# First layer's down projection as seven half-size products; weight sums spread two at a time; three norms from sums by token

## The chip, the cores and the metric

The kernel runs on one core of one Trainium2 chip. The metric is device time in microseconds; the kernel before took 1694.76 us (median of three runs, 1693.58 to 1695.71). Matrix products run on TensorE (PE), elementwise work on VectorE (DVE), ScalarE (ACT) and GpSimd (POOL); weights come in through DMA queues that SyncE (SP), POOL and ACT feed.

## What is computed

Two layers over 512 tokens of width 1024, in float32:

```python
for l in range(DEPTH):                      # DEPTH = 2
    h = rmsnorm(x, norm1_g[l])
    p = h @ w_in[l]                         # split for three branches and their gates
    y_rw, y_ret, y_sg = rwkv7(...), retention(...), spatial_gating(...)
    x = x + sum(gates * branch_projections) @ w_out[l]          # "output projection"
    u = rmsnorm(x, norm2_g[l]) @ ffn_w_up[l]                    # "up projection", 2 * 2816 columns
    c = causal depthwise convolution of width 3 over u
    gate, val = split(c)
    x = x + (silu(gate) * val) @ ffn_w_down[l]                  # "down projection", K = 2816
return rmsnorm(x, final_g)
```

## The kernel before, in words

The activations lie with channels on the 128 partitions and the 512 tokens along the free dimension. Every large product is made of float32 values split in two parts of a reduced format, `hi` and `lo` (one ACT copy and one DVE subtraction each, `part`, lines 140 and 141), and of three matmuls per 128 x 128 block (`mm3`, lines 153 to 163): `hi*lo`, `hi*hi`, `lo*hi`. Weights come as units of at most 128 x 512 elements (256 KB), read by SP (`load`, line 127), split by `part`, and used by TensorE. `unit` walks a plan of all units in advance: it reads up to `NRAW` or `DEEP` units ahead and splits as many ahead as `AHEAD` gives for the unit's pool. A scheduler orders the instructions of each engine from its own timing model, except where `keep_in_program_order` pins them (`self.pin` for matmuls, `self.keep` for splits and norms).

The stages of a layer are: the mixer (three branches), the output projection (`wout`: eight row blocks `m`, each 8 x 3 matmuls of 512 columns, then `xi`, the residual sum, and the norm's pieces `norm_z` and `norm_sq`), the up projection (`ffn_up`: 44 columns of 8 x 3 matmuls, each followed by the scaling with the norm's factor row `rsF`, the convolution and the gate) and the down projection.

The second layer's down projection (`last`) is computed with seven products of half the size in each dimension (a Strassen scheme): the activations are combined by `halves` in the up projection, and the weight blocks by `presum`: four DMA loads of `wdt` on POOL's queue into `pre` tiles, four DVE sums, four DMA stores to DRAM (`ts`), which `last` reads back as units. Four of the seven products use such sums. `presum` for the second layer runs during the up and down projection of the first. The first layer's down projection (`ffn_down`, lines 1146 to 1160) is a plain product: for each of eight row blocks 22 x 3 matmuls of 512 columns, with the activations split by `split`.

A norm needs the sum of squares over channels of each token. For the first norm of the program this is done by `norm_stats` (four matmuls with one output column, a DVE step, a POOL power, giving the factor by token) and `norm_rows` (four transposes on TensorE and one ACT copy, giving the row `rsF`). The other three norms use `norm_bcast` (lines 282 to 300): the squares are split, two matmuls of 512 columns with a matrix of ones sum and spread them, and ACT's square root and four DVE reciprocals give `rsF`; for the second layer's first norm a DVE transpose and POOL copies also give the factor by token. `firstF` (lines 318 to 330) places it: three columns are begun with the first half of the channels, then the norm, then the second halves.

Of the kernel before, what the change touches and what calls it, by code (L numbers as in the profile page):

```python
# [8 lines left out]
F32 = mybir.dt.float32  # L9
# [6 lines left out]
L = 2  # L16
# [10 lines left out]
PRE = {(0, "f", 2): 0, (0, "f", 4): 1, (0, "f", 6): 2, (0, "f", 8): 3, (0, "d", 0): 4, (0, "d", 1): 5, (0, "d", 2): 6, (0, "d", 3): 7,  # L27
       (0, "d", 4): 8, (0, "d", 5): 9, (0, "d", 6): 10}
# [24 lines left out]
class Emit:  # L53
# [41 lines left out]
    def unit(self, name, l, i, c0, n=512):  # L95
# [9 lines left out]
        while self.npart < len(self.plan):  # L105
# [6 lines left out]
            while self.nraw < len(self.plan) and self.nraw < self.npart + (DEEP if self.plan[self.nraw][5] in ("q", "u") else NRAW):  # L112
                self.load(self.plan[self.nraw])
# [8 lines left out]
    def load(self, u):  # L122
        name, l, i, c0, n, _ = u
        raw = self.u(n="wr") if u[5] in ("q", "u") and self.nraw % 2 else self.wp.tile([128, 512], F32, name=self.nm("wr"), tag="wr", bufs=NRAW)
        src = self.tsum[i] if name == "tsum" else self.a[name][l, i]
        with self.tc.high_priority():
            self.kept(self.nc.sync.dma_start(raw[:, :n], src[:, c0:c0 + n]))
        self.raws.append(raw)
        self.nraw += 1

    def part(self, u):
# [5 lines left out]
        else:  # L137
            hi, lo = [{"f": self.f, "r": self.r, "u": self.u, "p": self.u, "q": self.u}[pool](dt=F32R, n=t) for t in ("sh", "sl")]
# [104 lines left out]
    def presum(self, l, stage, m):  # L243

        if self.pre:
            q, b = self.pre.pop()
            V = self.nc.vector
            V.tensor_tensor(b[3], b[3], b[1], op=SUB)
            V.tensor_tensor(b[1], b[1], b[0], op=SUB)
            V.tensor_tensor(b[0], b[0], b[3], op=ADD)  # L250
            V.tensor_tensor(b[2], b[2], b[0], op=SUB)
            for p, t in zip((7, 5, 6, 4), (b[3], b[1], b[0], b[2])):
                self.tsum[q, p] = self.dp.tile([128, 512], F32, name=self.nm("ts"))
                self.nc.gpsimd.dma_start(self.tsum[q, p], t)
        q = PRE.get((l, stage, m))
        if q is not None:
            b = self.fpre.pop(0) if stage == "f" else [self.u(n="pre") for _ in range(4)]
            for i, t in enumerate(b):
                self.nc.gpsimd.dma_start(t, self.a["wdt"][0, 2 * q + i // 2][:, i % 2 * 512:i % 2 * 512 + 512])
            self.pre.append((q, b))  # L260
# [20 lines left out]

    def norm_bcast(self, st, cols):

        nc, po = self.nc, self.tc.keep_in_program_order
        hi, lo = st["sq"]
        pb = self.sm()
        po(nc.tensor.matmul(pb, self.ones, lo, start=True, stop=False))
        po(nc.tensor.matmul(pb, self.ones, hi, start=False, stop=True))
        rms = self.u(n="rms")
        nc.scalar.activation(rms, pb, AF.Sqrt, scale=1.0 / D, bias=self.c("eps"))  # L290
        self.rsF = self.small((128, 512), "rsF", bufs=1)
        for c in range(NC):
            cs = slice(c * 128, c * 128 + 128)
            nc.vector.reciprocal(self.rsF[:, cs], rms[:, cs])
        if cols:
            t = self.u((128, 4, 4, 32), n="rst")
            nc.vector.transpose(t.rearrange("p c b r -> p (c b r)"), self.rsF)
            self.rsT = self.small((128, 4), "rs")
            for b in range(4):
                nc.gpsimd.tensor_copy(self.rsT[32 * b:32 * b + 32, :], t[32 * b:32 * b + 32, :, b, 0])  # L300
# [1166 lines left out]
```

## Time and profile before

| | |
|---|---|
| median of three runs | 1694.76 us |
| the profiled execution | 1695.1 us |
| span of its profile | 1693.4 us |
| TensorE matmuls | busy 1683.6 us (99%), 10247 instructions |
| TensorE weight loads | busy 1382.6 us (82%), overlapping the matmuls |
| VectorE | busy 1218.0 us (72%) |
| ScalarE | busy 794.9 us (47%) |
| GpSimd | busy 261.8 us (15%) |
| DMA | 260.01 MB, mean 154 GB/s |

A matmul's duration in the profile runs from its issue to its modelled end, so consecutive matmuls overlap in the records; what a matmul costs in a stream is the distance between two starts. In the rows, `a<-b,c` names the result first, then the streamed operand and the loaded weights; `128x512` is the shape of the result. Times in windows and timelines count from the span's start.

The places on TensorE, from the timeline: the first layer's output projection is interleaved with the last of the mixer and ends near 494.6 us, its norm's sum stands at 506.7 us; the first down projection ends near 854.3 us, with the norm's sum at 862.3 us; the second layer's `xi` rows run from before 1321.7 to 1343.8 us and its norm's sum stands at 1353.7 us; the last down projection runs to 1687 us.

### The profile page before, as it was taken

Reading aid. Unit: us, or ns where it says so; the run is one execution under the profiler, and the core shown is the slowest. Engines: PE = TensorE matmul, PEld = TensorE weight load, DVE = VectorE, ACT = ScalarE, POOL = GpSimd, SP = SyncE. Lnnn points to the kernel's source line nnn. Section 1 sums busy time; section 2 is a strip of 40 time slices with the busy share of each in tenths; the row PEclk is TensorE's granted clock in tenths of the full one; section 3 lists DMA queues with packets and bytes.
Section 4 is the critical chain, followed back from the end, with each engine's and each line's share of the span. In section 5 each row is a group of like instructions: output and inputs, shape, how many; then the busy total and the mean of one; then the engine's idle time right before and its main releaser. Section 6 shows DMA issues by size and latency. Waiting matters only on the chain.

```text
span 1693.4 us, 27939 instructions
## 1 busy us (share of the span) xinstructions
PE 1683.6 (99%) x10247; PEld 1382.6 (82%) x10247; DVE 1218.0 (72%) x2114; ACT 794.9 (47%) x1366; POOL 261.8 (15%) x376
## 2 busy tenths in 40 slices
PE   9999999999999999999999999999999999999998
PEld 7888877888888888888888888778888888888887
DVE  7887745578669877655568888465786688887777
ACT  6563543554255444433346544335542544444555
POOL 1121000303301200003321210003132012220000
PEclk9999999999999999999999999999999999999999
DMA  5236553625544533147743265536255434443775
GB/s 182 87 108 204 181 176 96 191 84 163 190 144 149 193 125 94 63 146 265 246 147 95 94 206 184 178 98 190 83 164 165 153 97 143 143 140 112 242 241 178
DMA packets 143529, 260.01 MB, mean 154 GB/s; under 512 B 19584, under 2 KB 35584, under 8 KB 143392
## 3 DMA queue, kind: packets, MB, share of 16 engines
q1 hardware_dynamic: 117200, 188.67, 35.5%
q0 software_dynamic: 17552, 54.15, 9.8%
q10 hardware_dynamic: 8640, 15.42, 2.5%
q8 instruction: 80, 1.31, 0.3%
q14 instruction: 57, 0.47, 0.1%
HBM read 212.94 MB, written 45.22 MB: 152 GB/s over the span
## 4 chain that ended last, share of the span: by engine, by line
PE 94%; issue 4%; DVE 1%; DMA 0%; POOL 0%; ACT 0%; DVEq 0%; POOLq 0%; ACTq 0%
PE acc L157 85%; PE sm L157 3%; PE sm L683 2%; PE sm L937 1%; PE sm L590 1%; PE sm L1045 0%; PE acc L351 0%; PE sm L553 0%; PE sm L552 0%; PE sm L965 0%; PE sm L992 0%; DMA s<-wl 0%; PE sm L837 0%; DVE wl L141 0%; PE sm L828 0%
## 5 line engine op out<-in xcount | busy, mean ns | idle before, releaser
L157 PE MATMUL acc<-lo,sh 128*128 128x512 f32 x1108 | 431.9, 390 | 0.0
L157 PE MATMUL acc<-hi,sh 128*128 128x512 f32 x1108 | 431.9, 390 | 0.0
L157 PE MATMUL acc<-hi,sl 128*128 128x512 f32 x1108 | 424.8, 390 | 0.0
L140 ACT CAST sh<-wr 128x512 fp32r<-128x512 f32 (+1 forms) x375 | 226.6, 614 | 298.9 <-PE acc L157 163.0
L141 DVE TENSOR_TENSOR sl<-wr,sh 128x512 fp32r<-128x512 f32 (+1 forms) x375 | 253.5, 683 | 99.8 <-ACT sh L140 70.1
L141 DVE TENSOR_TENSOR wl<-wr,wh 128x512 fp32r<-128x512 f32 x238 | 169.4, 715 | 145.2 <-ACT wh L140 142.2
L140 ACT CAST wh<-wr 128x512 fp32r<-128x512 f32 x238 | 146.8, 619 | 243.7 <-PE acc L157 151.8
L157 PEld LDWEIGHTS acc<-lo,sh 128*128 128x128 f32 x1108 | 208.0, 188 | 43.7 <-issue 0.9
L157 PEld LDWEIGHTS acc<-hi,sl 128*128 128x128 f32 x1108 | 208.1, 188 | 43.6 <-DVE gth L1060 0.3
L157 PEld LDWEIGHTS acc<-hi,sh 128*128 128x128 f32 x1108 | 208.1, 188 | 43.3 <-issue 0.3
L157 PE MATMUL acc<-lo,wh 128*128 128x512 f32 x588 | 231.7, 394 | 0.0
L157 PE MATMUL acc<-hi,wl 128*128 128x512 f32 x588 | 229.8, 391 | 0.0
L157 PE MATMUL acc<-hi,wh 128*128 128x512 f32 x588 | 229.2, 390 | 0.0
L1111 ACT ACTIVATE cv<-fu,pc 128x512 f32<-128x512 f32 x88 | 71.7, 816 | 139.4 <-DVE fu L1109 139.3
L157 PEld LDWEIGHTS acc<-hi,wl 128*128 128x128 f32 x588 | 110.4, 188 | 24.7 <-issue 0.9
L157 PEld LDWEIGHTS acc<-lo,wh 128*128 128x128 f32 x588 | 110.4, 188 | 24.3 <-ACT wh L140 0.6
L157 PEld LDWEIGHTS acc<-hi,wh 128*128 128x128 f32 x588 | 110.4, 188 | 22.4 <-issue 0.2
L157 PE MATMUL acc<-ah,sh 128*128 128x512 f32 x352 | 108.3, 389 | 0.0
L1112 DVE SCALAR_TENSOR_TENSOR cv<-fu,pc,cv 128x511 f32<-128x511 f32 x88 | 65.9, 750 | 34.8 <-ACT cv L1111 33.9
L157 PE MATMUL acc<-wl,hi 128*128 128x512 f32 x212 | 85.8, 405 | 0.0
L1109 DVE TENSOR_TENSOR fu<-acc,rsF 128x512 f32<-128x512 f32 x88 | 60.4, 686 | 31.8 <-PE acc L157 30.8
L157 PE MATMUL acc<-wh,hi 128*128 128x512 f32 x212 | 82.5, 389 | 0.0
(359 smaller groups left out, 2448.1 us busy)
## 6 DMA issues: line engine op xcount, KB each, us to landing
wr<-wall SPq DMA_DIRECT2D x480, 256.0 KB, 2.8
gd<-gth ACTq DMA_DIRECT2D x48, 256.0 KB, 3.2
gth<-gd POOLq DMA_DIRECT2D x48, 256.0 KB, 3.3
pre<-wdt POOLq DMA_DIRECT2D x44, 256.0 KB, 5.6
ts<-pre POOLq DMA_DIRECT2D x44, 256.0 KB, 2.8
wr<-ts SPq DMA_DIRECT2D x44, 256.0 KB, 4.2
wr<-wdn SPq DMA_DIRECT2D x40, 256.0 KB, 3.9
wr<-wdt SPq DMA_DIRECT2D x33, 256.0 KB, 4.2
```

Source lines behind the costliest of these rows:

```text
L140: self.kept(self.nc.scalar.copy(hi[:, :n], raw[:, :n]))
L141: self.kept(self.nc.vector.tensor_tensor(lo[:, :n], raw[:, :n], hi[:, :n], op=SUB))
L157: i = self.nc.tensor.matmul(*x, **y, **kw)
L590: i = T.matmul(pK[hv[1 - h], j, :], bk[hv[h], c, 1, :], x[hv[h], c, :], start=True, stop=True)
L683: po(T.matmul(o, l, r, start=start, stop=True, skip_group_check=True))
L937: po(T.matmul(X[h][:, i, :], lhsT, rhs, start=new[h], stop=stop, skip_group_check=True))
L1109: V.tensor_tensor(u, ps, self.rsF, op=MUL)
L1111: A.activation(t, u, AF.Identity, scale=self.p("cw2", j), bias=self.p("cb", j))
L1112: V.scalar_tensor_tensor(t[:, 1:], u[:, :511], self.p("cw1", j), t[:, 1:], op0=MUL, op1=ADD)
```

## The change

1. The first layer's down projection becomes seven products of half size. The weights stay the loaded operand; each matmul streams 256 columns. The results are added into the residual tiles `x[m]` in place, in halves of 256 columns.
2. `presum` becomes a generator `sums` for each layer, stepped two sums at a time in the output projection (`m` 1 to 6) and the up projection (`i` 0 to 15) of the same layer; the first layer needs it now too.
3. `halves` is used in both layers' up projections, and splits and norms there are pinned in both. The code that reads back the combined activations (`kit`) is shared by both.
4. `norm_bcast` is gone: the three norms use `norm_stats` and, two steps later in `firstF`, `norm_rows`.
5. Units of the output projection get the pool `w` and those at the end of the first down projection the pool `k`: half of the raw tiles come from the pool `f`, and more of them are read and split ahead.

```diff
-AHEAD = {None: 2, "p": 4, "r": 3, "f": 3, "u": 5, "q": 4}
+WOS, UPS = range(1, 7), range(16)
+AHEAD = {None: 2, "p": 4, "r": 3, "f": 3, "u": 5, "q": 4, "k": 5, "w": 3}
...
+    def sums(self, l):
+        V, P, Q = self.nc.vector, self.nc.gpsimd, NFF // 2
+        def get(q):
+            b = [self.f(n="pre") for _ in range(4)]
             for i, t in enumerate(b):
+                P.dma_start(t, self.a["wdt"][l, 2 * q + i // 2][:, i % 2 * 512:i % 2 * 512 + 512])
+            return b
+        b = get(0)
+        yield
+        for q in range(Q):
+            n = get(q + 1) if q < Q - 1 else None
+            for p, o, x, op in ((7, 3, 1, SUB), (5, 1, 0, SUB), (6, 0, 3, ADD), (4, 2, 0, SUB)):
+                V.tensor_tensor(b[o], b[o], b[x], op=op)
+                self.tsum[l, q, p] = self.dp.tile([128, 512], F32, name=self.nm("ts"))
+                P.dma_start(self.tsum[l, q, p], b[o])
+                if p == 5:
+                    yield
+            b = n
+            yield
...
         for i, g in enumerate(gs + gs):
             if i == at:
-                self.norm_bcast(st, l and ids[0] == 12)
+                self.norm_stats(st)
+            elif i == at + 2:
+                self.norm_rows()
             next(g)
...
     def wout(self, l, mg, xd, st):
+        self.sum, self.pool = self.sums(l), "w"
+        self.presum()
         for m in range(8):
...
+            self.presum(m in WOS)
+        self.pool = "r"
...
         for i in range(NFF):
-            if l == 0 and i % 2 == 0 and 2 <= i <= 10:
-                self.presum(l, "f", i)
+            self.presum(i in UPS)
...
-            if l < L - 1:
-                act.append(self.split(th, at))
-            elif i % 2 == 0:
+            if i % 2 == 0:
                 even = th
             else:
                 pair = [even, th]
...
     def ffn_down(self, l, act, x, st):
-        for m in range(8):
-            ps = self.acc()
-            self.matF(ps, ("wdn", l, m, 0), act)
-            V.scalar_tensor_tensor(x[m], ps, 0.5, x[m], op0=MUL, op1=ADD)
-            self.norm_z(st, x[m], "n1")
-            self.norm_sq(st, x[m])
...
+        def prod(ps, x, at, w, first, end, ms=range(4)):
+            for m in ms:
+                c = slice(128 * m, 128 * m + 128)
+                self.mm3(ps[m // 2][:, H[m % 2]], (w[0][:, c], w[1][:, c]), (x[0][:, at:at + 256], x[1][:, at:at + 256]),
+                         first and m % 2 == 0, end, skip_group_check=True)
+        def plus(m, h, ps, i):
+            V.scalar_tensor_tensor(x[m][:, H[h]], ps[i // 2][:, H[i % 2]], 0.5, x[m][:, H[h]], op0=MUL, op1=ADD)
...
+        for q in range(Q):                                   # Q = 11
+            for p in (7, 5, 6, 4) if q < Q - 1 else (6, 7, 5, 4):
+                w = unit(p, q)
+                side(n)
+                n += 1
+                xs, at = {7: (t, 0), 5: (s, 0), 6: (s, 256), 4: (t, 256)}[p]
+                prod(pss[p], xs, at, w, q == 0, q == Q - 1)
...
+        for q in range(Q):
+            w = unit(1, q)
+            rest(q)
+            prod(out[1], ab[q], 0, w, False, q == Q - 1)
...
+        for q in range(Q):
+            w = unit(2, q)
+            prod(out[2], ab[q], 256, w, q == 0, q == Q - 1)
...
+        for q in range(Q - KEPT):                            # KEPT = 6
+            w = unit(3, q)
+            prod(out[3], s4[q // 2], q % 2 * 256, w, q == 0, False)
...
+            if q:
+                norm(q - 1)
+        self.pool = "k"
+        ws = [unit(3, q) for q in range(Q - KEPT, Q)]
+        for b in range(2):
+            ms = (2 * b, 2 * b + 1)
+            for q, w in enumerate(ws, Q - KEPT):
+                prod(out[3], s4[q // 2], q % 2 * 256, w, False, q == Q - 1, ms)
+            for i in ms:
+                plus(4 + i, 0, out[3], i)
+            for i in ms:
+                norm(4 + i)
```

How the order of instructions moves is shown at three places; all are in the first layer, and the second has the same pattern. In the rows, `xi` takes a finished row block out of PSUM and adds the residual, `lo` and `sq` are the norm's pieces, `sl` is the second part of a split weight unit, `pre` a weight sum, `acc` a result in PSUM.

The first place is VectorE in the output projection, where row block 3 leaves PSUM. Before:

```order
L1074 SCALAR_TENSOR_TENSOR xi_5127<-acc_5129,xi_5127 128x512
L141 TENSOR_TENSOR sl_5368<-wr_5318,sh_5367 128x512
L221 SCALAR_TENSOR_TENSOR lo_5168<-xi_5127,pc_175,hi_5167 128x512
L228 TENSOR_TENSOR sq_5171<-sq_5124,sq_5171 128x512
L141 TENSOR_TENSOR sl_5386<-wr_5336,sh_5385 128x512
L1074 SCALAR_TENSOR_TENSOR xi_5174<-acc_5176,xi_5174 128x512
```

Now, from the previous block's `xi` (`xi_5155`, block 2) to that of block 3 (`xi_5208`), the last 9 of 14 rows:

```order
L227 TENSOR_TENSOR sq_5199<-sq_5138,sq_5199 128x512
L257 TENSOR_TENSOR pre_5364<-pre_5364,pre_5363 128x512
L140 TENSOR_TENSOR sl_5501<-wr_5451,sh_5500 128x512
L257 TENSOR_TENSOR pre_5363<-pre_5363,pre_5366 128x512
L257 TENSOR_TENSOR pre_5607<-pre_5607,pre_5605 128x512
L257 TENSOR_TENSOR pre_5365<-pre_5365,pre_5363 128x512
L140 TENSOR_TENSOR sl_5519<-wr_5480,sh_5518 128x512
L257 TENSOR_TENSOR pre_5605<-pre_5605,pre_5604 128x512
L1063 SCALAR_TENSOR_TENSOR xi_5208<-acc_5210,xi_5208 128x512
```

Eight sums and one more weight split (`sl_5519`) now stand ahead of `xi_5208`; of the 44 sums of a layer, 24 stand in the output projection, 18 of them between the first and the fourth `xi`.

The second place is TensorE where row block 6 ends and row block 7 begins, which is the same in both kernels but for the names. Now:

```order
L156 MATMUL acc_5379<-lo_5037,sh_5321 128x512
L156 MATMUL acc_5379<-hi_5036,sh_5321 128x512
L156 MATMUL acc_5379<-hi_5036,sl_5322 128x512
L156 MATMUL acc_5432<-lo_4727,sh_5339 128x512
L156 MATMUL acc_5432<-hi_4726,sh_5339 128x512
L156 MATMUL acc_5432<-hi_4726,sl_5340 128x512
```

The third row is the last use of the unit `sh_5321`/`sl_5322`. The 16 tiles of the pool `r` hold eight split units, so the eighth unit after it, `sh_5518`/`sl_5519`, is written into its tiles. `acc_5432` goes into the PSUM bank of `acc_5210` (four banks in rotation), which `xi_5208` empties.

The third place is VectorE in the second half of the output projection. Before:

```order
L1074 SCALAR_TENSOR_TENSOR xi_5221<-acc_5223,xi_5221 128x512
L141 TENSOR_TENSOR sl_5437<-wr_5383,sh_5436 128x512
L221 SCALAR_TENSOR_TENSOR lo_5262<-xi_5221,pc_175,hi_5261 128x512
L228 TENSOR_TENSOR sq_5265<-sq_5218,sq_5265 128x512
L1074 SCALAR_TENSOR_TENSOR xi_5268<-acc_5270,xi_5268 128x512
L141 TENSOR_TENSOR sl_5455<-wr_5416,sh_5454 128x512
```

Now:

```order
L140 TENSOR_TENSOR sl_5564<-wr_5516,sh_5563 128x512
L227 TENSOR_TENSOR sq_5309<-sq_5252,sq_5309 128x512
L140 TENSOR_TENSOR sl_5589<-wr_5543,sh_5588 128x512
L1063 SCALAR_TENSOR_TENSOR xi_5318<-acc_5320,xi_5318 128x512
L220 SCALAR_TENSOR_TENSOR lo_5357<-xi_5318,pc_175,hi_5356 128x512
L227 TENSOR_TENSOR sq_5360<-sq_5309,sq_5360 128x512
L140 TENSOR_TENSOR sl_5649<-wr_5561,sh_5648 128x512
L257 TENSOR_TENSOR pre_5694<-pre_5694,pre_5692 128x512
L1063 SCALAR_TENSOR_TENSOR xi_5377<-acc_5379,xi_5377 128x512
```

Block 5 was `xi_5268` and is `xi_5318`, block 6 is `xi_5377`. The splits ahead of them, `sl_5589` and `sl_5649`, go into the tiles of the units that the first halves of the first two columns of the up projection use last (`sl_5401`, `sl_5436`, each eight units earlier); the second and the third of these columns (`acc_5478`, `acc_5479`) go into the PSUM banks that `xi_5318` and `xi_5377` empty. Before, `xi_5268` stood ahead of `sl_5455`.

Around the norm, TensorE had two 512-column matmuls (`sm_5470<-lo_5410,ones` and `sm_5470<-hi_5409,ones`); it now has four with one output column (`sm_5534<-con,sq_5474`) and, 24 matmuls later, four transposes (`sm_5579<-con,rs_5541`). The same holds for the other two norms.

More of the change, by code (lines that the diff above doesn't have):

```diff
@@ L280, in norm_rows @@
         self.nc.scalar.copy(self.rsF, pb)
[L282 to L300, printed above, removed]
     def firstK(self, st):
@@ L1101, in ffn_up @@
             cs = []
-            self.keep = l == L - 1 and i > 1
+            self.keep = i > 1
             for j in (i, NFF + i):
@@ L1160, in ffn_down @@
+        self.pin = self.keep = False
         return x, xd
```

148 lines of the change are left out of this document (81 added, 67 removed).

## The prediction

> **What bounds the kernel now.** I read the page's busy rows and chain first, then the chain's longest piece, then the waits of TensorE.
>
> ```profile
> PE 1683.6 (99%) x10247; PEld 1382.6 (82%) x10247; DVE 1218.0 (72%) x2114; ACT 794.9 (47%) x1366; POOL 261.8 (15%) x376
> ...
> PEclk9999999999999999999999999999999999999999
> ...
> PE 94%; issue 4%; DVE 1%; DMA 0%; POOL 0%; ACT 0%; DVEq 0%; POOLq 0%; ACTq 0%
> ```
>
> ```profile
> 507.27 355.19 PE acc L157 x1567
> ```
>
> ```profile
> PE acc L351 <- DVE rst L348: 1.5, 1, 1.5
> PE sm L590 <- issue: 0.8, 1, 0.8
> PE sm L607 <- ACT Y L595: 0.5, 1, 0.5
> ```
>
> TensorE is busy 99% of the span at its full clock and holds 94% of the chain; its waits sum to little more than these 2.8 us. From 507 to 862 us it runs 1567 matmuls without a break, 0.2267 us from start to start. So every matmul saved counts, and every wait put into this stream counts in full. VectorE, at 72%, has no such price of its own: it matters where TensorE waits for it.
>
> **The down projection.** Before, it is 8 x 22 x 3 = 528 matmuls:
>
> ```profile
> L157 PE MATMUL acc<-ah,sh 128*128 128x512 f32 x352 | 108.3, 389 | 0.0
> ...
> L157 PE MATMUL acc<-ah,sl 128*128 128x512 f32 x176 | 68.5, 389 | 0.0
> ```
>
> 528 x 0.2267 = 119.7 us. Now it is 7 products x 11 units x 4 column groups x 3 = 924 matmuls of 256 columns, each with a weight load of its own. The last product of the second layer has such a stream:
>
> ```profile
> 1682.71 0.28 PE L157 MATMUL acc<-sl,hi 128*128 128x256 f32 x1
> ...
> 1686.91 0.28 PE L157 MATMUL sm<-sh,lo 128*128 128x256 f32 x1
> ```
>
> These are the first and the last of 36 rows, 35 distances: 4.20 / 35 = 0.1200 us. 924 x 0.1200 = 110.9, so **-8.8 us**. (The Trainium skill, page "TensorE: Matmul & The Clock Gate", section "Back-to-back issue gap", gives an isolated gap of N / 2.4 + 2.5 ns, that is 215.8 and 109.2 ns; by it the term would be 113.9 - 100.9, -13.0 us. The rows measure both, 226.7 and 120.0, so -8.8 stands.) Its additions and splits keep ahead of TensorE by the order: between the first use of a product's weights and the matmul that last freed their tiles lie at least 39 matmuls of 256 columns, 4.7 us, against cast and split of 1.3 us. I add 0.5 us for its start, bounded by nothing and by 1.
>
> **The norms.** Two forms stand in the trace:
>
> ```profile
> 22.77 0.95 PE L269 MATMUL sm<-con,sq 128*128 128x1 f32 x8
> ...
> 24.37 0.40 PE L157 MATMUL acc<-lo,wh 128*128 128x512 f32 x1
> ...
> 26.44 0.60 PE L278 MATMUL sm<-con,rs 128*128 128x128 f32 x4
> ...
> 27.34 0.40 PE L157 MATMUL acc<-hi,wl 128*128 128x512 f32 x1
> ```
>
> From 22.77 to 24.37 are 1.60 us with three 512-column matmuls in them: 0.92 for the sums; from 26.44 to 27.34 are 0.90 with two: 0.45 for the transposes. That row has eight sums, now there are four (0.5 is the low bound). The two matmuls with ones cost 2 x 0.2267 = 0.45. Three norms: 3 x (0.92 + 0.45 - 0.45) = **+2.75 us**, at least 1.5. The chain behind the sums has 24 matmuls (5.4 us) of cover, against about 2 us of small steps, and four reciprocals leave VectorE.
>
> **The sums of weights.** They are 44 more on VectorE, and 24 per layer now stand in the output projection. There the first four row blocks are finished nearly together, and block m (4 to 7), then the up projection's first columns, reuse the four PSUM banks in turn: each start waits until `xi` has emptied its bank. These are VectorE's rows there now, with the cast and the matmul:
>
> ```profile
> 469.91 0.69 DVE L1074 SCALAR_TENSOR_TENSOR xi<-acc,xi 128x512 f32<-128x512 f32 x1 [0.42 <-PE acc L157]
> ```
>
> ```profile
> 487.22 0.69 DVE L228 TENSOR_TENSOR sq<-sq,sq 128x512 f32<-128x512 f32 x1
> 487.82 0.69 DVE L1074 SCALAR_TENSOR_TENSOR xi<-acc,xi 128x512 f32<-128x512 f32 x1
> 488.42 0.68 DVE L141 TENSOR_TENSOR sl<-wr,sh 128x512 fp32r<-128x512 f32 x1
> 489.30 0.75 DVE L221 SCALAR_TENSOR_TENSOR lo<-xi,pc,hi 128x512 fp32r<-128x512 f32 x1 [0.20 <-ACT hi L220]
> 489.97 0.69 DVE L228 TENSOR_TENSOR sq<-sq,sq 128x512 f32<-128x512 f32 x1
> ```
>
> ```profile
> 478.34 0.62 ACT L140 CAST sh<-wr 128x512 fp32r<-128x512 f32 x1 [0.57 <-ACT sq L226]
> ```
>
> ```profile
> 478.78 0.39 PE L157 MATMUL acc<-hi,sl 128*128 128x512 f32 x1
> ```
>
> ```profile
> L250 DVE TENSOR_TENSOR pre<-pre,pre 128x512 f32<-128x512 f32 x11 | 7.6, 690 | 0.2
> ...
> L140 ACT CAST sh<-wr 128x512 fp32r<-128x512 f32 (+1 forms) x375 | 226.6, 614 | 298.9 <-PE acc L157 163.0
> ...
> L157 PEld LDWEIGHTS acc<-hi,sl 128*128 128x128 f32 x1108 | 208.1, 188 | 43.6 <-DVE gth L1060 0.3
> ```
>
> A step of VectorE is 0.60 us (0.67 after a `lo`), an `xi` is done after 0.69, a sum is like any of them, a cast takes 0.62, a matmul's record ends 0.39 after its start. The cast's group is the point (the last row, of the weight loads, is for a rival): casts wait for TensorE to give back a tile, 163.0 us in all, and that has been free, because nothing TensorE wanted stood behind them. The order shows that this changes. `xi_5208` (block 3, whose bank block 7 needs) stands behind `sl_5519`, whose tile the last matmul of block 6 gives back; `xi_5318` and `xi_5377` stand behind splits whose tiles the matmul just ahead of the needy column gives back. Each is a **closed loop**: matmul, cast, split, perhaps a sum, `xi`, next matmul. With no sum it takes, from the last matmul's start, 0.16 + 0.62 + 0.60 + 0.69 = 2.07 us (0.16 is the end of the matmul before it) instead of 0.23: 1.84 us lost; with a sum 2.44; four hand-overs add some 0.1.
>
> I follow VectorE's queue with these steps. Block 0 ends four matmuls later than in the row above (470.8). From the first to the second `xi` the steps just fit. Block 5 gives its half's tile back at 481.7; cast, `sl_5454`, three sums, `xi_5155` end at 485.5, and block 6 could have begun at 484.2: 1.3 lost. Block 6 ends at 491.0; cast, split (VectorE is at 492.1 with its eight sums), a sum, `xi_5208` to 494.0: 3.0. `xi_5269` is early. Second column: 502.2, to 504.3: 2.1. Third: 507.05, to 509.75: 2.7. Fourth: five steps after that `xi`, 512.5 to 513.4: 0.9. The first layer loses **10.0 us**. The second layer's order, in the same way, gives 2.6 and 1.2 (blocks 6 and 7), 1.9, 2.5 and 0.4 (columns): **8.6 us**. Nothing hides this: TensorE has no other work in its queue there. The low bound is the six closed loops alone at 1.84, 11.0 us.
>
> The transfers: in these stages come some 19 MB per layer (weights 4.2, `xi` 2.1, loads and stores of the sums 6.3 each) in about 54 us, 350 GB/s, where a saturated window moves 336:
>
> ```profile
> 1600.00:1610.00 10.00, 10.00 (x46) 8.29 (x45) 8.67 (x14) 6.93 (x13) 0.00 (x0) 1.00 1.00 336
> ```
>
> ```profile
> pre<-wdt POOLq DMA_DIRECT2D x44, 256.0 KB, 5.6
> ...
> xi<-xT SPq DMA_DIRECT2D x8, 256.0 KB, 3.3
> ```
>
> SP issues each `xi` load behind a weight load that waits for a split. With 3.3 us to landing blocks 5 and 6 have 1.1 us to spare and block 7 none; with the 5.6 us of the sums' loads they would lose about 1.2, 1.2 and 2.3 a layer. I take none of it and keep +9 for the range. In the up projection twenty sums of 0.60 are spread over some 20 columns of 5.44 us, 11% more for VectorE, which in the second layer was at 82%:
>
> ```profile
> 1440.00:1480.00 40.00, 40.00 (x179) 33.11 (x178) 32.86 (x54) 17.39 (x29) 8.32 (x16) 1.00 0.47 145
> ```
>
> That makes 93%, just under; I take nothing, and +4 as the bound.
>
> **The sum.** 1695.1 (profiled execution) - 8.8 + 0.5 + 2.75 + 10.0 + 8.6 = 1708.2; the execution is 0.3 above the median, so **1708 us**.
>
> **Rivals.** (1) *TensorE stays unbroken; faster.* If VectorE got to each `xi` in time, the sum is 1695.1 - 8.8 + 0.5 + 2.75 - 0.3 = 1689.3. For it: TensorE never waits in these stages now, with the same tiles. It decides by one point, whether the `xi` passes the waiting split; a queue that executes in the written order can't let it, and I see no row where VectorE overtook. (The Trainium skill, same page, section "Architectural detail: the array is 16x 32x32, not 1x 128x128", says that VectorE and ScalarE are strict first-in first-out and that TensorE alone pulls weight loads ahead. By that rule the loops are closed and the time is 1708; without it 1689. In the trace VectorE sits 0.20 for a `lo` at 489.30 rather than start the next row, which agrees.) 7%. (2) *The gain and a part of the loops cancel; no change.* With only the three loops of one layer, 5.5 us plus hand-overs, the time is 1695. It needs the other layer's splits to be early; its order shows the same rows. 6%. (3) *The weight loads pace the narrow matmuls.* At their 0.188 each the down projection would be 173.7 us, and the time 1771; against it are the 36 rows at 0.120, since the page counts as many loads as matmuls. 1%. (4) *The transfers come late too*: 1708 + 9 = 1717. For it the 350 against 336 GB/s; against it, weights are read up to six units ahead. 14%.
>
> **How the numbers follow.** My forecast, all closed loops and no more than 4 us beside them, has 72%. The low bounds (six loops at 1.84, norms at 1.5) give 1708 - 7.6 - 1.25 = 1699; the transfers give 1717. That is the range, 1699 to 1717; it leaves out rivals 1 and 3, most of 2 and a little above 4. A measurement here tells 0.2%, 3.4 us, from no change: faster (below 1691.4) 7%, within 6%, slower 87%.
>
> **What would show it.** In the changed kernel's waits of TensorE, `acc` behind DVE `xi` of the output projection (line 1063) should have about ten entries of 0.4 to 3 us, 15 to 20 us in all, five of them in each layer; a window over 484 to 514 us should show TensorE some 10 us short. The down projection should be an unbroken stream at 0.120; each norm 1.4 us of TensorE. If these `xi` waits are missing, the prediction is wrong and rival 1 holds; if their releaser is a DMA, rival 4.

## The result, and the profile after

The changed kernel takes **1732.07 us** (median of five runs, 1729.14 to 1733.3) against 1694.06 before (median of five, 1693.58 to 1695.71): ratio 1.0216, 95% interval 1.0204 to 1.0228. The forecast was 1708, range 1699 to 1717: the direction was right, the size was not. The profiled execution has a span of 1727.4 us (before 1693.4) and took 1729.14, the lowest of the five; the 2.9 us up to the median are in no trace and stay unassigned.

From the page of the changed kernel, the busy times, the row of TensorE in 40 slices and the shares of the chain:

```profile
PE 1691.3 (98%) x10673; PEld 1401.8 (81%) x10673; DVE 1278.2 (74%) x2269; ACT 808.9 (47%) x1410; POOL 330.4 (19%) x496
...
PE   9999999999979999999999999999999799999998
...
PE 85%; issue 4%; DVE 4%; DMA 3%; POOL 1%; ACT 1%; SPq 0%; DVEq 0%; POOLq 0%; ACTq 0%
```

TensorE is now idle for 36.1 us of the span (9.8 before), 19 us of it in two slices, which are the two output projections, and it is 7.7 us longer busy although 528 long matmuls became 924 short ones. Both have to be explained. TensorE's waits:

```profile
PE acc L156 <- DVE xi L1063: 20.1, 9, 3.3
PE acc L156 <- ACT sh L139: 3.1, 2, 2.5
PE acc L156 <- DVE sl L140: 2.9, 4, 1.8
```

The first row is the forecast one: nine waits of a product for the `xi` that empties its bank, 20.1 us in all, and no releaser that is a DMA. The next rows were not forecast.

**First output projection.** The window that the prediction named, before and now (length, then busy time of PE, PEld, DVE, ACT, POOL, granted clock, DMA share, GB/s):

```profile
484.00:514.00 30.00, 30.00 (x134) 24.86 (x133) 22.10 (x34) 15.85 (x26) 0.00 (x0) 1.00 0.39 128
```

```profile
484.00:514.00 30.00, 21.93 (x83) 16.71 (x82) 22.96 (x38) 10.55 (x17) 9.04 (x17) 0.90 0.79 282
```

Its longest wait, and what follows it, in TensorE's timeline (start, duration; in brackets the idle time before and its releaser):

```profile
491.54 0.39 PE L156 MATMUL acc<-hi,sl 128*128 128x512 f32 x1
494.69 0.76 PE L156 MATMUL acc<-lo,sh 128*128 128x512 f32 x1 [2.76 <-DVE xi L1063]
495.25 0.63 PE L156 MATMUL acc<-hi,sh 128*128 128x512 f32 x1
...
497.38 0.63 PE L156 MATMUL acc<-lo,sh 128*128 128x512 f32 x1
```

and, ahead of that `xi`, a cast of ScalarE and VectorE's rows:

```profile
491.78 0.62 ACT L139 CAST sh<-wr 128x512 fp32r<-128x512 f32 x1 [2.10 <-PE acc L156]
```

```profile
490.25 0.68 DVE L140 TENSOR_TENSOR sl<-wr,sh 128x512 fp32r<-128x512 f32 x1
490.85 1.89 DVE L257 TENSOR_TENSOR pre<-pre,pre 128x512 f32<-128x512 f32 x3
492.65 0.68 DVE L140 TENSOR_TENSOR sl<-wr,sh 128x512 fp32r<-128x512 f32 x1
493.26 0.69 DVE L257 TENSOR_TENSOR pre<-pre,pre 128x512 f32<-128x512 f32 x1
493.86 0.68 DVE L1063 SCALAR_TENSOR_TENSOR xi<-acc,xi 128x512 f32<-128x512 f32 x1
```

This is the chain that the prediction followed for block 7: the last matmul of block 6 at 491.54, the cast that waited for TensorE at 491.78, the split at 492.65, a sum, `xi` at 493.86 (predicted end 494.0, measured 494.54), the matmul at 494.69. But the cast was done at 492.40, and VectorE worked without a gap until 492.65: what came last here was its own full queue, three sums of it, and the loop just ahead of that. Ahead of block 6's wait (1.04 us), too, VectorE has no gap. Closed loops with an idle VectorE are the fourth and the fifth wait, those of the second and the third column:

```profile
505.15 0.69 DVE L140 TENSOR_TENSOR sl<-wr,sh 128x512 fp32r<-128x512 f32 x1 [1.32 <-ACT sh L139]
...
510.03 0.69 DVE L140 TENSOR_TENSOR sl<-wr,sh 128x512 fp32r<-128x512 f32 x1 [1.45 <-ACT sh L139]
```

The first wait (1.52 us, block 5) was not forecast. A cast ahead of its `xi` waited for a weight load, and VectorE 0.48 us for that cast:

```profile
476.76 0.62 ACT L139 CAST sh<-wr 128x512 fp32r<-128x512 f32 x1 [2.05 <-DMA wr<-wall]
```

What the prediction did not have at all stands below the wait of block 7: matmuls of 512 columns start **0.427 us** apart instead of 0.227 until 497.8. That is half clock; it is why the window above has a granted clock of 0.90. The same is behind the fifth wait of this stage (2.46 us).

**Second layer.** Two of its waits, again in TensorE's timeline, and the `xi` that released the first of them, in VectorE's:

```profile
1363.14 0.50 PE L156 MATMUL acc<-lo,sh 128*128 128x512 f32 x1 [3.28 <-DVE xi L1063]
1368.63 0.79 PE L156 MATMUL acc<-lo,sh 128*128 128x512 f32 x1 [2.48 <-DVE xi L1063]
```

```profile
1362.39 0.69 DVE L1063 SCALAR_TENSOR_TENSOR xi<-acc,xi 128x512 f32<-128x512 f32 x1 [1.38 <-DMA xi<-xd]
```

That `xi` itself sat 1.38 us for its load: in this layer the transfers are late too. So were weight loads ahead of the `xi` of the 1.45 us wait, where VectorE sat 0.88 and 0.53 us for casts:

```profile
1329.92 0.62 ACT L139 CAST sh<-wr 128x512 fp32r<-128x512 f32 x1 [1.77 <-DMA wr<-wall]
```

**Second up projection**, which was forecast to lose nothing:

```profile
1432.09 0.50 PE L156 MATMUL acc<-lo,sh 128*128 128x512 f32 x1 [2.53 <-ACT sh L139]
1435.13 0.80 PE L156 MATMUL acc<-hi,sl 128*128 128x512 f32 x1 [1.78 <-DVE sl L140]
```

```profile
1431.91 0.69 DVE L257 TENSOR_TENSOR pre<-pre,pre 128x512 f32<-128x512 f32 x1 [1.24 <-DMA pre<-wdt]
```

An addition at the head of VectorE's queue waited 1.24 us for its own block to land, and the split for which TensorE waits at 1435.13 stood behind it. (The cast behind the 2.53 us stood on ScalarE behind an activation that had waited 1.69 us for VectorE.) Ten matmuls at 0.427 follow the one at 1435.13.

**First down projection**, from its first to its last matmul:

```profile
749.20:860.60 111.40, 111.09 (x926) 110.89 (x925) 85.03 (x158) 63.54 (x113) 4.28 (x8) 1.00 0.71 233
```

111.4 us at full clock with one wait of 0.31, forecast 110.9 + 0.5. **Norms**, one of the three:

```profile
521.77 0.95 PE L276 MATMUL sm<-con,sq 128*128 128x1 f32 x8
...
528.16 0.60 PE L285 MATMUL sm<-con,rs 128*128 128x128 f32 x4
```

TensorE does not wait at either of the two. The row has eight sums, as the one that the prediction read.

### The profile page after: what moved, and what is told of

Its sections match the earlier page's. It is cut to its first block, busy times and chain, and to the rows that moved or that the text cites. A ratio compares the mean times of both kernels' runs of the same rounds, so it can differ in the third digit from the quotient of the medians.

```text
span 1727.4 us, 29345 instructions
## 1 busy us (share of the span) xinstructions
PE 1691.3 (98%) x10673; PEld 1401.8 (81%) x10673; DVE 1278.2 (74%) x2269; ACT 808.9 (47%) x1410; POOL 330.4 (19%) x496
## 3 DMA queue, kind: packets, MB, share of 16 engines
q8 instruction: 84, 1.38, 0.3%
## 4 chain that ended last, share of the span: by engine, by line
PE 85%; issue 4%; DVE 4%; DMA 3%; POOL 1%; ACT 1%; SPq 0%; DVEq 0%; POOLq 0%; ACTq 0%
PE acc L156 74%; PE sm L156 5%; PE sm L670 2%; DMA wr<-wall 1%; PE sm L924 1%; DVE sl L140 1%; DMA pre<-wdt 1%; DVE pre L257 1%; PE sm L577 1%; PE sm L1032 0%; POOL gth L1044 0%; DVE cv L1100 0%; POOL ts L259 0%; ACT sh L139 0%; DMA tr<-xT 0%
## 5 line engine op out<-in xcount | busy, mean ns | idle before, releaser
L156 PE MATMUL acc<-lo,sh 128*128 128x512 f32 (+1 forms) x1156 | 451.3, 390 | 24.7 <-DVE xi L1063 20.1
L156 PE MATMUL acc<-hi,sh 128*128 128x512 f32 (+1 forms) x1156 | 448.6, 388 | 0.0
L156 PE MATMUL acc<-hi,sl 128*128 128x512 f32 (+1 forms) x1156 | 437.6, 389 | 2.3 <-DVE sl L140 2.2
L140 DVE TENSOR_TENSOR wl<-wr,wh 128x512 fp32r<-128x512 f32 x281 | 196.0, 702 | 165.5 <-ACT wh L139 160.2
L139 ACT CAST sh<-wr 128x512 fp32r<-128x512 f32 x361 | 215.4, 615 | 195.7 <-DMA wr<-wall 87.5
L140 DVE TENSOR_TENSOR sl<-wr,sh 128x512 fp32r<-128x512 f32 x361 | 243.9, 689 | 71.8 <-ACT sh L139 63.5
L156 PE MATMUL acc<-lo,wh 128*128 128x512 f32 (+1 forms) x628 | 243.4, 388 | 0.0
L156 PE MATMUL acc<-hi,wl 128*128 128x512 f32 (+1 forms) x628 | 241.1, 384 | 0.0
L156 PE MATMUL acc<-hi,wh 128*128 128x512 f32 (+1 forms) x628 | 240.5, 383 | 0.0
L156 PE MATMUL acc<-wh,lo 128*128 128x512 f32 x212 | 82.5, 389 | 0.0
```

The source lines that it names most:

```text
L139: self.kept(self.nc.scalar.copy(hi[:, :n], raw[:, :n]))
L140: self.kept(self.nc.vector.tensor_tensor(lo[:, :n], raw[:, :n], hi[:, :n], op=SUB))
L156: i = self.nc.tensor.matmul(*x, **y, **kw)
```

## Experiments

Ratios are to the kernel before on the same chip, in brackets the 95% interval. The theory is the prediction's: the *order* in which the sums' presence puts `xi` behind splits (closed loops). Its rivals are the additions' own time on VectorE and the sums' transfers.

**e2: no sums.** The products that want a sum read a plain block, so they multiply other numbers; everything else is the change.

```diff
-                return self.unit("tsum", l, (q, p), 0)
+                return self.unit("wdt", l, 2 * q + (p in (4, 6)), 512 * (p in (6, 7)))
-        self.sum, self.pool = self.sums(l), "w"
-        self.presum()
+        self.sum, self.pool = iter(()), "w"
```

> Left out: the sums of weight blocks (no loads, additions or stores of them in either layer); the four products that want sums read plain weight blocks of the same size instead, in both layers. Everything else of the change is there, the narrow down projection and the norms by token. Every theory that puts the loss on the sums expects what is left of the prediction's own terms: 1694.1 - 8.3 (the stream as it measured) + 2.75 + 0.5 = 1689, no wait of TensorE for xi, and no matmuls at half clock. A theory that puts part of the loss on the down projection, the norms or the new pools of weight units expects more than 1695.

1691.94 us, 0.9982 [0.9972, 0.9991]. There is no `xi` wait at all. The sums cost all of the loss; what is left gains 0.2%, not quite the 0.3% worked out.

**e3: order pinned.** All sums stay; in `wout`, loads and splits and the `xi` step keep the program's order, so that no split whose tile comes back late stands ahead of an `xi`.

```diff
+        self.keep = True
-            V.scalar_tensor_tensor(xi, ps, 0.5, xi, op0=MUL, op1=ADD)
+            self.tc.keep_in_program_order(V.scalar_tensor_tensor(xi, ps, 0.5, xi, op0=MUL, op1=ADD))
-        self.pool = "r"
+        self.pool, self.keep = "r", False
```

> All sums, all transfers; only the order is changed: in the output projection xi, the weight loads and the splits keep the order in which the code writes them, so that each xi stands ahead of the splits whose tiles are given back late. Theory 1 (the order: xi behind a split that waits for TensorE closes a loop) expects the xi waits of the first layer (9.6 us) and its half-clock stretches (about 4 us) to go, most of the second layer's 15.7 us too, and the up projection's 9.6 us to stay: 1732 - 13 - 13 = 1706, at most 1712. Theory 2 (the transfers of the sums make weights and xi late, the order only shows it) expects the same transfers to cost the same: at least 1724, with xi waiting for its own load.

1703.64 us, 1.0052 [1.0037, 1.0067]. The same additions and transfers, another order, and three quarters of the loss are gone (1.0216 - 1.0052 = 0.0164, 28 us). The `xi` waits are gone. Up to five sums still stand between two `xi`, but no split there waits for more than 0.28 us, and the `xi` steps are spread: the first stands at 459.57 us, in the changed kernel at 471.33. So this run shows that the order makes the loss there; it does not tell closed loops from a full queue. Its longest waits are now

```profile
PE acc L156 <- DVE sl L140: 5.1, 7, 1.7
PE acc L156 <- ACT sh L139: 3.4, 2, 2.6
```

mostly in the second up projection, where again an addition holds VectorE's queue for its block:

```profile
1404.83 0.69 DVE L257 TENSOR_TENSOR pre<-pre,pre 128x512 f32<-128x512 f32 x1 [1.17 <-DMA pre<-wdt]
```

TensorE's two waits next to it, at 1405.08 and 1408.04, are 2.55 and 1.66 us, and twelve matmuls at 0.427 follow.

**e5: order pinned, additions left out** (the blocks are read and stored unadded).

```diff
-                V.tensor_tensor(b[o], b[o], b[x], op=op)
```

> Left out: the additions on VectorE; the blocks are loaded and stored back as they are, so all transfers of the sums remain, and the order in the output projection is pinned as in the run before. Theory 1 expects next to no loss, 1692 (1689 and a few us where a load is late). Theory 2 (transfers) expects most of the loss to stay, 1715 or more, with casts waiting for weight loads. Theory 3 (VectorE has no room for 88 more steps) expects 1690, since VectorE has its room back.

1696.61 us, 1.0009 [1.0000, 1.0018]: the 88 reads and 88 stores cost 4.7 us over e2, nearer to theory 1's 1692 than to theory 2's 1715, and no matmul runs at half clock.

**e6: transfers left out, additions kept**, 44 in each layer, order not pinned.

> Left out: the transfers of the sums; one set of blocks per layer is loaded, all 44 additions per layer are done on it, nothing is stored, and the products read plain weight blocks. By the order no xi stands behind a split that waits for the last matmuls, though two to four additions stand ahead of each xi. Theory 1 expects no closed loop and so 1690 to 1695. Theory 2 expects 1689 to 1692. Theory 3 (VectorE's time) expects 1705 or more, with waits of TensorE in the up projections.

1706.67 us, 1.0068 [1.0053, 1.0083]. The theory of the order had 1690 to 1695 here, that of VectorE's time 1705 or more. The size is the latter's, but the waits are not in the up projections, where it had them; `xi` waits return, smaller:

```profile
PE acc L156 <- DVE xi L1061: 7.2, 6, 1.9
```

No VectorE row ahead of these late `xi` waits for anything: the additions alone, in the changed kernel's order, fill its queue.

Brought to one place in the order of matmuls (0.2267 us for each that stands ahead), the profiled executions compare with e2 stage by stage, in us:

| stage | changed kernel | e3 pinned | e5 pinned, transfers only | e6 additions only |
|---|---|---|---|---|
| to the first layer's second norm | +12.9 | -1.0 | -1.5 | +4.2 |
| to the second layer's first norm | -0.1 | +0.2 | -0.2 | +1.8 |
| to the second layer's second norm | +13.6 | -0.9 | -1.3 | +2.5 |
| to the end | +7.2 | +9.9 | +0.8 | +1.3 |

(In the third row e2 has a wait of 1.85 us and some half clock of its own. Each column is one execution: e2's profiled one is its slowest, 3.6 us above its median, e5's its fastest, 3.2 below. So e5 looks 6.7 us cheaper here than by its median, and no trace says in which row.) The output projections lose to the order, part of it to additions alone (+4.2 and +2.5). In these executions the second up projection loses much **only when additions and transfers come together**.

**e14: the sums' steps four blocks later in the up projection**, order pinned.

```diff
-WOS, UPS = range(1, 7), range(16)
+WOS, UPS = range(1, 7), range(4, 20)
```

> The changed kernel with the order of the output projection pinned as in e3_kept (1703.64 us), and the sums' steps in the up projections at blocks 4 to 19 instead of 0 to 15. In e3_kept the second layer's up projection lost some 9.7 us, its first waits (2.55 and 1.66 us, and 11 matmuls at half clock) in the first blocks behind the norm, with neither transfers alone nor additions alone losing them. Theory, the loss is a crowding of VectorE and the weights' transfers in the blocks just behind the norm: most of it goes, 1695 to 1699. Rival, the crowding moves along with the sums: 1702 to 1706.

1699.03 us, 1.0017 [1.0008, 1.0026]: 5.9 us better than e3 (by the ratios). The waits of e3 shrink to

```profile
PE acc L156 <- DVE sl L140: 2.7, 5, 0.7
PE acc L156 <- ACT sh L139: 1.7, 1, 1.7
```

and no addition of the up projections waits for its transfer, and no matmul there runs at half clock. Placed as in the table above, its last stage is 3.1 us over that of e2, where e3's is 9.9. So the crowd behind the norm was the cause of most of it; it does not simply move along. This is the best full version of the change, and still not faster than before.

**e10: order pinned, additions on GpSimd.**

```diff
-                V.tensor_tensor(b[o], b[o], b[x], op=op)
+                P.tensor_tensor(b[o], b[o], b[x], op=op)
```

> The changed kernel with the order of the output projection pinned as in e3_kept, and the 88 additions of the sums moved from VectorE to GpSimd. All transfers stay. e3_kept is 1703.64 us, and without additions it was 1696.61 (e5_dma_kept). Theory: what the additions cost beyond the closed loops is VectorE's time in the second layer's up projection: 1703.6 - 7.0 = 1696.6. Rival: the additions cost through what they do to the transfers or through GpSimd's own lateness (each takes over 1.4 us there, and GpSimd issues the sums' transfers too): 1702 to 1708.

1770.14 us, 1.0442 [1.0427, 1.0456]: the theory of a free VectorE fails badly, and the rival's 1702 to 1708 falls far short too. The groups on VectorE and GpSimd (busy us, mean ns):

```profile
L1102 DVE SCALAR_TENSOR_TENSOR cv<-fu,pc,cv 128x510 f32<-128x510 f32 x88 | 92.5, 1052 | 2.3
L1098 DVE TENSOR_TENSOR fu<-acc,rsF 128x512 f32<-128x512 f32 x88 | 59.9, 681 | 25.7 <-ACT rsF L287 19.6 <-PE acc L156 6.0
L220 DVE SCALAR_TENSOR_TENSOR lo<-xi,pc,hi 128x512 fp32r<-128x512 f32 x24 | 32.8, 1367 | 11.9 <-ACT hi L219 11.9
```

```profile
L257 POOL TENSOR_TENSOR pre<-pre,pre 128x512 f32<-128x512 f32 x88 | 116.6, 1329 | 14.9 <-DMA pre<-wdt 13.4
```

In e3, with the additions on VectorE, the same three were

```profile
L1102 DVE SCALAR_TENSOR_TENSOR cv<-fu,pc,cv 128x510 f32<-128x510 f32 x88 | 65.6, 747 | 1.8
L1098 DVE TENSOR_TENSOR fu<-acc,rsF 128x512 f32<-128x512 f32 x88 | 60.2, 685 | 22.2 <-PE acc L156 12.6 <-ACT rsF L287 9.3
L220 DVE SCALAR_TENSOR_TENSOR lo<-xi,pc,hi 128x512 fp32r<-128x512 f32 x24 | 17.9, 747 | 3.6 <-ACT hi L219 3.6
```

An addition takes 1.33 us on GpSimd, and VectorE instructions with two SBUF tensors that run beside it take up to twice their time in the mean (`lo` 747 to 1367 ns; one split, at 495.98, took 6.71 us, with four additions of GpSimd beside it), while `fu`, which reads one of its two from PSUM, keeps its 0.68 us. So VectorE lost more than it was spared: it is busy 1327.5 us without the additions, 1277.6 with them in e3, and TensorE's waits for its splits grew from 5.1 to 37.0 us. (The Trainium skill, page "SBUF — State Buffer", section "SBUF: two separate sides", says that GpSimd shares a port pair with VectorE under a lock held for a whole instruction, and that VectorE operations with two SBUF inputs are caught by it; these rows agree.)

**e8, e9, e11: the norm as before the change**, put back into e3, e2 and e10.

```diff
-                self.norm_stats(st)
-            elif i == at + 2:
-                self.norm_rows()
+                self.norm_bcast(st, l and ids[0] == 12)
...
+            st["sq"] = self.split(st["acc"])
```

> The changed kernel with the order of the output projection pinned as in e3_kept, and in addition the norm as it was before the change (two matmuls on the squares' two parts, root and reciprocal, instead of sums by token). It prices the three new norms alone, beside e3_kept's 1703.64 us. Theory of the prediction (each new norm 0.92 us dearer on TensorE): 1703.64 - 2.75 = 1700.9. Rival A, the new norm's wait is hidden by the two products put between its halves: 1703.6. Rival B, the old norm's chain (squares, split, root, four reciprocals) comes late when VectorE also does the additions: 1704 to 1706.

e8: 1713.98 us, 1.0109 [1.0095, 1.0123], that is 9.7 us *slower* than e3 with the new norm (by the ratios). The old norm needs a split of the squares, and with the additions VectorE comes late to it, as rival B had it, though for more than its 1704 to 1706:

```profile
PE sm L294 <- DVE lo L149: 7.9, 2, 4.1
```

> The changed kernel without the sums of weights (the products that need them read plain blocks of the weights instead, so those products are of other numbers) and with the norm as it was before the change. What is left of the change is the first down projection by seven half-size products. Beside e2_no_sums (1691.94 us) it prices the norms where VectorE is free: by the prediction 1691.94 - 2.75 = 1689.2, a gain over before of 5.5; rival, norms cost nothing where VectorE is free: 1691.9.

e9 (no sums, other numbers as in e2): 1695.67 us, 0.9999 [0.9991, 1.0008]. No gain over before is left, and it is 0.17% above e2. Its norms wait for nothing, but new single waits stand elsewhere in its order, the longest 2.60 us for `sh` at 881.0, 1.39 for `S` at 1099.3, 1.35 for `wl` at 1590.9 and 1.30 each for `sl` at 748.9 and `gth` at 1296.0.

> Pinned order, additions on GpSimd, and the norm as it was before the change: the whole down projection by seven products with the sums, computed in full, and nothing else of the change on the path. If the additions' cost is VectorE's time and the norms' is 2.75: 1696.6 - 2.75 = 1693.9, level with before (1694.75) or just below it. Rival, GpSimd is late with the sums: 1699 to 1705.

e11: 1781.64 us, 1.0512 [1.0491, 1.0533]; the additions on GpSimd hide any price of the norm.

**e13: the kernel before with the new norm alone.**

> The kernel before with the new norm alone (sums by token for the three norms; down projection, sums of weights and order as before). By the prediction each of the three costs TensorE 0.92 us more: 1694.8 + 2.75, ratio 1.0016. Rival, from e9_no_sums_old_norm beside e2_no_sums (1.0 to 1.5 us dearer on TensorE by its norm-to-norm stretch, but no splits of the squares on ScalarE and VectorE, and no reciprocals ahead of the first products' use): level with before or up to 3 us faster, ratio 0.998 to 1.000.

1698.46 us, 1.0015 [1.0006, 1.0024]: +2.5 us (1.0 to 4.1), beside the forecast 2.75. The rival, drawn from e9, falls: where nothing else changes, the new norm is dearer by what was worked out. Where VectorE is full it is the cheaper one (e8).

**e12: nine pauses** put into the first down projection of e2.

```diff
+    def pause(self, ps, k):
+        po = self.tc.keep_in_program_order
+        po(self.nc.tensor.matmul(ps[:, :96], self.ones, self.zz, start=False, stop=False, skip_group_check=True))
+        for _ in range(k):
+            po(self.nc.vector.tensor_tensor(self.zz, self.rst[:, :96], self.rst[:, :96], op=SUB))
+        po(self.nc.tensor.matmul(ps[:, :96], self.ones, self.zz, start=False, stop=False, skip_group_check=True))
...
+                if q and n % 4 == 2 and n < 41:
+                    self.pause(pss[p][0], (4, 7, 10, 13, 16)[n // 4 % 5])
```

> The kernel of e2_no_sums (no sums of weights, 1691.94 us) with nine pauses of TensorE put into the first down projection, some 10 us apart: in each, TensorE waits for 7, 10, 13, 16, 4, 7, 10, 13 and 16 small VectorE instructions (128 x 96, 0.26 us each by the rows of 256 and 512 columns: pauses of about 1.0, 1.8, 2.6, 3.4 and 4.2 us) and adds zeros. Theory, half clock: behind some pauses, none of those under 2 us and most of those over 3.4, the matmuls of 256 columns start 0.24 us apart instead of 0.120, for at most 3.4 us, so that such a pause costs up to 1.7 us more than its length: 25 us of pauses and up to 10 more, 1720 to 1728. Rival, a pause costs its length alone and the half clock in the changed kernel comes from something else there: 1717 to 1719 and no matmul at 0.24.

1745.36 us, 1.0302 [1.0284, 1.0319]; span 1741.8 against 1693.8 in e2, 48.0 more. The pauses came out longer than set, since other VectorE work stood between the small instructions. All nine, in TensorE's timeline:

```profile
751.17 0.45 PE L1179 MATMUL acc<-zz,ones 128*128 128x96 f32 x1 [5.92 <-DVE zz L1178]
...
762.10 0.45 PE L1179 MATMUL acc<-zz,ones 128*128 128x96 f32 x1 [2.98 <-DVE zz L1178]
...
773.59 0.45 PE L1179 MATMUL acc<-zz,ones 128*128 128x96 f32 x1 [3.86 <-DVE zz L1178]
...
786.89 0.45 PE L1179 MATMUL acc<-zz,ones 128*128 128x96 f32 x1 [4.74 <-DVE zz L1178]
...
796.85 0.31 PE L1179 MATMUL acc<-zz,ones 128*128 128x96 f32 x1 [1.23 <-DVE zz L1178]
...
805.13 0.31 PE L1179 MATMUL acc<-zz,ones 128*128 128x96 f32 x1 [2.11 <-DVE zz L1178]
...
815.76 0.31 PE L1179 MATMUL acc<-zz,ones 128*128 128x96 f32 x1 [2.98 <-DVE zz L1178]
...
827.29 0.45 PE L1179 MATMUL acc<-zz,ones 128*128 128x96 f32 x1 [3.86 <-DVE zz L1178]
...
839.51 0.45 PE L1179 MATMUL acc<-zz,ones 128*128 128x96 f32 x1 [4.74 <-DVE zz L1178]
```

They sum to 32.4 us. Most of the other 16 is half clock, some 12.5 us (134 matmuls, 0.093 each); the rest is about what nine waits cost beside their length (0.25 each, below). Behind eight of the nine, all but the 1.23, matmuls of 256 columns start 0.213 us apart instead of 0.120, as in the rows 806.85 to 809.41, until some 2.9 to 5.7 us after the pause's end. Windows behind the 4.74, the 1.23 and the 2.11 us pause (length, then as above):

```profile
788.00:790.00 2.00, 2.00 (x11) 2.00 (x11) 1.85 (x4) 0.00 (x0) 0.00 (x0) 0.50 0.63 166
797.00:799.00 2.00, 2.00 (x18) 2.00 (x19) 0.40 (x1) 0.42 (x1) 0.00 (x0) 1.00 0.18 63
808.00:809.00 1.00, 1.00 (x7) 1.00 (x7) 0.43 (x1) 0.00 (x0) 0.00 (x0) 0.50 0.99 377
```

Behind the 2.11 pause TensorE first ran 1.3 us at full clock and was halved then. Pauses make the half clock; the rival falls.

What decides is where a pause falls, more than its length. In every trace with several stretches at half clock they start on one grid of 3.41 us and last whole steps of it, up to the trace's end. In the changed kernel they start at 494.63, 511.69, 1344.55, 1368.44 and 1433.29, that is 0, 5, 249, 256 and 275 steps of 3.413 us from the first. Three of its steps:

```profile
504.87:508.28 3.41, 1.78 (x8) 1.48 (x9) 2.34 (x4) 1.49 (x3) 0.00 (x0) 1.00 0.48 171
508.28:511.69 3.41, 1.25 (x6) 0.69 (x4) 1.96 (x4) 0.62 (x1) 0.07 (x1) 1.00 0.07 27
511.69:515.11 3.42, 3.13 (x7) 2.48 (x8) 3.39 (x7) 1.24 (x2) 1.85 (x4) 0.50 0.89 302
```

In the first TensorE stood idle for 1.63 us, and the next is at full clock; in the second for 2.16, and the next is at half. Over all thirteen traces, between the first 20 and the last 25 us, each step with 2.0 us idle or more was followed by half clock, and no step at full clock with less than 1.3 idle was. Between the two both happen: the wait of 1.65 us in e14, at 1302.50, was followed by it, and that of 2.60 in e9, which lies across two steps (1.86 and 0.74), was not.

(The Trainium skill, page "TensorE: Matmul & The Clock Gate", section "What's actually happening", says that activity is judged in free-running windows of 3.4 us and that the clock halves after one idle window. The late halving and the grid fit windows that don't start with the pause; a whole idle window does not fit: pauses of 2.11 and 2.98 us, shorter than a window, were enough.)

## Why the prediction was right and wrong

The order of the queues was read rightly, the sum was too small, and part of the agreement in the first layer is luck. Forecast against the profiled executions, in us; each wait of *w* on the page costs *w* + 0.25, since the matmul ahead of it would have been followed 0.16 before its record ends, and the first one behind takes some 0.09 longer (479.46 to the next is 0.31):

| term | forecast | measured |
|---|---|---|
| down projection with its start | -8.3 | -8.3 (111.4 against 119.7) |
| norms | +2.75 | +2.5 (e13) |
| first output projection, waits | +10.0 | +10.8 (five `xi` waits, 9.59, + 5 x 0.25) |
| second output projection, waits | +8.6 | +14.1 (six waits, 12.55, + 6 x 0.25) |
| second up projection, waits | 0 | +5.5 (three waits, 4.76, + 3 x 0.25) |
| matmuls at half clock | not there | +8.0 (14 + 15 + 11 of them, 0.20 each) |
| sum | +13.05 | +32.6; spans +34.0 |

The `xi` waits and their like by place, forecast and measured (each *w* + 0.25), in us; the columns are the first of the up projection:

| | first layer | second layer |
|---|---|---|
| block 5 | 0, 1.8 | 0, 1.7 |
| block 6 | 1.3, 1.3 | 2.6, 3.6 |
| block 7 | 3.0, 3.0 | 1.2, 0.8 |
| second column | 2.1, 2.1 | 1.9, 3.5 |
| third column | 2.7, 2.7 | 2.5, 2.7 |
| fourth column | 0.9, 0 | 0.4, 0 |
| a gate's product (`gth`), ahead of block 5 | 0, 0 | 0, 1.7 |

1. **Down projection, norms, first layer's loops:** right in size. That the norm's row has eight sums "now there are four" was misread: there are eight in both, so its low bound of 0.5 had no ground. Four of the first layer's waits came as followed through the queue; that their total came within 0.8 is partly luck, since an unforecast wait for a late load in block 5 stands for the fourth column's that did not come. e3 shows that the order makes them; e6 shows that additions ahead of `xi` cost 7.2 us of waits even where no split waits, so the closed loops are not the whole of it, and the low bound, loops alone, prices only a part. The rivals that forecast no loss (1689, 1695) fall with the `xi` waits; the rule on strict queues that stood beside them holds: each late `xi` started behind the row ahead of it. The weight loads don't pace the narrow matmuls (111.4 us, not 173.7).
2. **Failed: "The first layer loses 10.0 us", and every other wait, priced at its length.** A TensorE that stands still for two to three microseconds can lose clock as well. Two of the first layer's five waits were followed by it; over the kernel it slowed 40 matmuls, some 8 us. The trace of before has no half clock in a long product, so this price had no row; it should have been an unknown with a bound. e12 measures it.
3. **Failed: "I take none of it and keep +9 for the range" (transfers).** In the second layer an `xi` waited 1.38 us for its load (second column), and late weight loads held the casts ahead of block 5's `xi`, as they did in the first layer. The layer's 8.6 became 14.1. Rival 4 was right in kind. That transfers set a wait is shown for these three; what made 3.6 of block 6's 2.6, and the wait for `gth`, was not tried.
4. **Failed: "just under; I take nothing, and +4 as the bound" (up projection).** A mean of 93% over 40 us says nothing of the first blocks behind the norm, where the additions meet late blocks and hold VectorE's queue. The loss was 5.5 in waits and 2.2 at half clock. In the traces of e5 and e6 neither part alone makes it (0.8 and 1.3 of 9.9, with the doubt on e5 said there), and e14 shows that starting the steps four blocks later removes most.
5. **The range** added these bounds up to one side only: +9 for the transfers was its end, and +4 and the clock were outside. All three came at once.

The remaining 1.4 us of the span's 34.0, and 2.9 between the profiled execution and the median, stay open. So does why e9 found nothing of the down projection's 8.3: its single waits (some 7.5 us over those of before) take the place of the gain, but why its order has them was not tried.

## What to carry to other kernels

Where TensorE is the bound, a new step on a strict queue costs not its own time but whatever then stands ahead of the instruction TensorE needs: look for loops that close through a tile it has just given back, count the steps ahead, and pin the needed instruction ahead of prefetch work. A pause of TensorE of some two microseconds or more is to be priced at its length plus what may follow at half clock: a stretch of 3.41 us costs some 1.6 us (3.41 x (1 - 0.227 / 0.427)), and behind long pauses two came. Waits spread over several steps of the grid can be cheaper than one of the same sum. A mean share of a busy engine is no bound: add up the work in the few blocks where it meets late transfers.

## What the runs showed of the hardware

- TensorE's clock halves in the middle of a kernel: 512 columns go from 0.227 to 0.427 us and 256 from 0.120 to 0.213, for up to 5.7 us behind pauses from 2.11 us up (e12); the single pauses of 1.85 us in e2, at 1293.19, and of 1.65 in e14 were also followed by such matmuls. Those of 1.04, 1.52 and 1.81 us in the changed kernel's first layer were not, nor that of 2.60 in e9. Half clock comes in whole steps of a grid of 3.41 us, behind each step with 2.0 us idle or more and behind some with 1.4 to 1.9.
- GpSimd at 1.33 us an addition slows VectorE beside it: `lo` 747 to 1367 ns, `cv` 747 to 1052, a single split up to 6.71 us, with no change for the operation that reads PSUM (e10).
- Additions alone and transfers alone cost the second up projection 1.3 and 0.8 us in their traces, together 9.9 (e6, e5, e3; e5's trace is 3.2 us below its median): an addition that waited 1.24 us for its block held every VectorE row behind it.
